# Swapped PSUM tags in one FFN, mixer norms by columns, operand sums inside the first group, a warm-up at the start, plain gates scaled a tile earlier, and the last but one root half a tile later

## The chip, the cores and the metric

The kernel runs on one core of a Trainium2 chip. The metric is the time of one execution on the device, in microseconds (us), less being better. A core has engines that run side by side, each with a queue of its own that it works through in order: TensorE (PE, matrix products out of SBUF into the PSUM banks; its weight loads are PEld), VectorE (DVE), ScalarE (ACT), GpSimd (POOL) and SyncE (SP, which here only issues loads and stores). They wait for each other through semaphores.

## The reference

Two blocks, each a half-weighted SwiGLU, a mixer and another half-weighted SwiGLU, all behind an RMSNorm; block 0 has mixer A (indexed sparse attention), block 1 mixer B (chunked gMLP). The sequence has 512 tokens of width 1024, the hidden width is 2816, all float32:

```
for i in range(2):
    h = h + 0.5 * swiglu(rmsnorm(h, norm_g[i, 0]), ffn_w_in[i, 0], ffn_w_out[i, 0])
    hn = rmsnorm(h, norm_g[i, 1])
    y = mixer_a(hn, ...) if i == 0 else mixer_b(hn, ...)
    h = h + y
    h = h + 0.5 * swiglu(rmsnorm(h, norm_g[i, 2]), ffn_w_in[i, 1], ffn_w_out[i, 1])
return rmsnorm(h, final_g)

def rmsnorm(x, g):  return x * rsqrt(mean(x * x) + EPS) * g
def swiglu(x, w_in, w_out):
    gate, up = split(x @ w_in)
    return (silu(gate) * up) @ w_out
```

## The kernel before

**Layout.** The activations stand transposed: `H[0..7]`, eight tiles of 128 features x 512 tokens. Every product is made of three matmuls on split operands: `xh`/`whi` hold the upper part of a number, `xl`/`wlo` the rest, and `mul3` (lines 366 to 368) issues hi x hi, lo x hi, hi x lo. Weights come in on SP's queue as `raw` (512 KB a load); ACT writes `whi` (line 183), DVE then `wlo` (line 186). The converted weights stand in a ring of three units of eight 128x128 pieces, so a unit's conversion waits until PE has left the unit three back.

**One FFN.** The first `group` makes four output tiles at once (gate and up of hidden tiles 0 and 1) in four banks, over eight slices k of the input: twelve matmuls a slice. Four `single`s make the gates and ups of hidden tiles 2 and 3 (banks `rest`). These two pairs of tiles are the "plain" ones: `plain_pairs` multiplies the gates by the norm's factor (DVE), applies Silu (ACT), and leaves the multiplication with the up tile and the split into `yh`, `yl` in a list `later`, of which `step` takes one. All other hidden tiles come from `two_pairs`, which forms a 2x2 block product from seven products instead of eight; its right-hand operands are sums of quarters of x that `sums(kp)` makes for kp = 0..3: two scalings into `m` (ACT, line 446), four subtractions into `u` (DVE, lines 448 to 451), a split into `th` (ACT, line 388) and `tl` (DVE, line 389). The products' banks are copied out at line 519 (ACT, into `u` and `m`). Then the output products follow, in groups and singles; `add` multiplies a finished bank by half the norm's factor (DVE line 642, `gate`), adds it to `h` (643), and the next stage's `xh`, `xl` and the sum of squares `sqacc` are made from it.

**PSUM.** Two tags, `acc` and `aux`, of four banks each. A new bank of a tag takes over the bank of that tag used longest ago and waits for its readers. The first FFN of block 1 ends on `acc` banks and the stage behind it begins on `acc` banks, as does the first FFN of block 1 behind the second of block 0.

**Norms.** The four FFNs use `scale_columns` (line 394: `sqacc` as the weights against one column of ones, so that token sums stand as four columns; a root of twelve small DVE operations) and `scale_rows` (line 402: back to a row per token, copied to `b` and to half of it, `rh`). The mixers use `token_scale` (lines 345 to 351: split `sqacc` into `ah` and `al`, two 512-column products, and a root on 128x512 tiles) and `as_columns`.

**Where x is built.** In FFN (0,0) `H` is still loading during the first group, and `behind` (lines 305 to 317) makes each slice's `xh`, `xl` and squares between the matmuls. There the sums follow one by one behind the singles; in the other three FFNs they stand in the first group at k = 5, 6, 7 and behind the first single.

**Order.** Nothing reorders: each engine works in the order in which the code issues its instructions. The last stage stores a 128-token tile at a time: `rest` (lines 1146 to 1151, two halves) and `store` (its root and its scaling, line 1161).

Of the kernel before, what the change touches and what calls it, by code (L numbers as in the profile page):

```python
# [19 lines left out]
P = 128  # L20
# [220 lines left out]
def tile_trunk(ctx: ExitStack, tc, specs_out, xT, wst, gT, gl, rel, onehot, bu, bv, lng, lnb, wspT, bsp, out):  # L241
# [21 lines left out]
    def bank(tag="acc"):  # L263
        return psum.tile([P, 512], F32, tag=tag, bufs=4, name=uname(tag))
# [5 lines left out]
    pad(const, 32)  # L270
    pad(small, 32)
# [68 lines left out]

    def token_scale(tag="aux"):

        ah = small.tile([P, S], F32R, tag="s0_512", bufs=1, name=uname("ah"))
        al = small.tile([P, S], F32R, tag="s1_512", bufs=1, name=uname("al"))
        nc.scalar.activation(ah, acc[0], AF.Copy)
        nc.vector.tensor_tensor(al, acc[0], ah.bitcast(F32), op=ALU.subtract)
        ps = bank(tag)
        mm(ps, ones_r, ah, start=True, stop=False)
        mm(ps, ones_r, al, start=False, stop=True)
        v = small.tile([P, S], F32, tag="ms", bufs=1, name=uname("ms"))  # L350
        nc.vector.tensor_scalar(v, ps, 1.0 / D, EPS, op0=ALU.mult, op1=ALU.add)
        return rsqrt(v, [P, S])

    def as_columns(rb):

        ps = bank("aux")
        for t in range(NT):
            nc.tensor.transpose(ps[:, t * P:(t + 1) * P], rb[:, t * P:(t + 1) * P], ident)
        c = small.tile([P, NT], F32, tag="rcol", bufs=1, name=uname("rcol"))
        nc.vector.tensor_copy(c, ps.rearrange("p (t q) -> p t q", q=P)[:, :, 0])  # L360
        return c

    def mul3(ps, w, x, first, last, **kw):
# [26 lines left out]

    def scale_columns(ps):

        for t in range(NT):
            mm(ps[:, t:t + 1], acc[0][:, t * P:(t + 1) * P], ones[:, :1], start=True, stop=True)
        v = small.tile([P, NT], F32, tag="vcol", bufs=1, name=uname("vcol"))
        nc.vector.tensor_scalar(v, ps[:, :NT], 1.0 / D, EPS, op0=ALU.mult, op1=ALU.add)
        return rsqrt(v, [P, NT])

    def scale_rows(rc, ps):
# [4 lines left out]
        rh = small.tile([P, S], F32, tag="ms", bufs=1, name=uname("rh"))  # L404
        nc.scalar.activation(rb, ps, AF.Copy)
        nc.scalar.activation(rh, ps, AF.Copy, scale=0.5)  # L406
        return rb, rh

    def ffn(layer, which, norm, finish, begin=None, hooks=None, aside=None, last=None):

# [6 lines left out]
        NJ = DFF // P  # L417
        KP = KD // 2
        n1, n2 = slice(0, HALF), slice(HALF, S)
        with tc.tile_pool(name=uname("ffn"), bufs=1) as fp:  # L420
# [59 lines left out]
            def step():  # L480
                for _ in range(min(1, len(later))):
                    later.pop(0)()
# [74 lines left out]
            def scale():  # L557
                R["ps"] = R.get("ps") or bank("aux")
                R["c"] = scale_columns(R["ps"])

# [4 lines left out]
            def hook(k):  # L565
                if hooks:
                    hooks[k]()
                elif k in (5, 7):
                    (scale if k == 5 else spread)()
                if k > 4 and not hooks:  # L570
                    sums(k - 5)
# [4 lines left out]
            rest = [bank("aux") for _ in range(2)]  # L576
            if not hooks:
                plain_pairs(banks, g[0])
            else:
                R["ps"] = bank("aux")  # L580
            single(rest[0], 2, KD, spec_in)
            sums(0) if hooks else sums(3)
            step()
# [5 lines left out]
            rest.append(bank("aux"))  # L589
            single(rest[2], 3, KD, spec_in)  # L590
            if hooks:
                spread()
                nc.vector.tensor_tensor(g[1][:, 0], rest[0], R["b"], op=ALU.mult)
                plain_pairs(banks, g[0])
                sums(2)
            step()
            rest.append(bank("aux"))
            single(rest[3], NJ + 3, KD, spec_in)
            if hooks:
                sums(3)  # L600
            flush()
            done, n_dp = 0, 0
            for ci, dps in enumerate(CHUNKS):
# [6 lines left out]
                for i in range(dps):  # L610
                    pair = PLAIN + 2 * n_dp
                    between = ()
                    if n_dp == 0:
                        between = [lambda: plain_pairs(rest, g[1], 1 if hooks else 0)]
                    if aside:
                        aside(n_dp)
                    if last and n_dp == sum(CHUNKS) - 1:
                        between = last[0](bank("acc"), gate_tile)
                    two_pairs(pair, "aux" if n_dp % 2 else "acc", between)
                    n_dp += 1  # L620
                flush()
                n_k = done - p0
                tag0 = "aux" if n_dp % 2 else "acc"
                tag1 = "acc" if n_dp % 2 else "aux"

# [55 lines left out]
    def mixer_a(dist, next_norm):  # L681
# [9 lines left out]
        with ExitStack() as stack:  # L691
# [11 lines left out]

            def scale():
                R["b"] = token_scale("acc")

            kw = bank()
            pq = [bank("aux") for _ in range(4)]
            group([kw] + pq, ["kw"] + [QI0 + P * i for i in range(4)], KD, spec_a, hooks={4: scale})
            rb = R["b"]  # L710
# [38 lines left out]
            with tc.tile_pool(name="mixai", bufs=1) as ip:  # L749
# [21 lines left out]
                for i, _ in enumerate(projections(range(1), "acc")):  # L771
                    if i != KD:
                        continue
                    rc = R["c"] = as_columns(rb)
                    nc.vector.tensor_scalar(rq, rc, P ** -0.5, None, op0=ALU.mult)
# [171 lines left out]
    def mixer_b(next_norm):  # L947
        with tc.tile_pool(name="mixb", bufs=1) as bp:
# [12 lines left out]
            with tc.tile_pool(name="mixbv", bufs=1) as vp:  # L961
# [8 lines left out]
                nc.gpsimd.affine_select(out=wT, in_=wT, compare_op=ALU.is_ge, fill=0.0, base=0,  # L970
                                        pattern=[[0, GROUPS], [1, P]], channel_multiplier=-1)
                for c in range(6):
                    tag = "aux" if c % 2 else "acc"
                    banks = [bank(tag) for _ in range(NT)]
                    for k in range(KD):
                        wh, wl = W.take(*[("b_w_in", (0,), k * P, [(0, BH + c * 512 + i * P, P)]) for i in range(4)])
                        for t in range(NT):
# [3 lines left out]
                            mm(banks[t], xh, wl, start=False, stop=k == KD - 1)  # L981
                        if c == 0 and k == 4:
                            R["b"] = token_scale()
                        if c == 0 and k == KD - 1:
                            R["c"] = as_columns(R["b"])
                        if c == 1 and k == 3:
# [110 lines left out]
    ffn(0, 1, 2, into(3))  # L1097
    ffn(1, 0, 3, into(4))
    mixer_b(5)


# [24 lines left out]
    def last_product(n_k, spec, y_parts, rc, temp):  # L1126
# [110 lines left out]
```

## Time and profile before

| | |
|---|---|
| median of 3 runs | 2111.97 us (2110.95 to 2118.17) |
| profiled execution, own time | 2112.86 us |
| its span (first to last instruction) | 2110.8 us |
| PE busy | 2076.8 us (98% of the span), 12208 matmuls |
| DVE busy | 1487.5 us (70%), 2044 instructions |
| ACT busy | 891.3 us (42%), 1151 instructions |
| POOL busy | 78.8 us (4%), 58 instructions |
| DMA | 209.7 MB, 99 GB/s on the mean |

The own time is 2.06 us more than the span; that part lies around the instructions. A matmul is counted busy from its start to the end of its drain, so that consecutive matmuls overlap; what one costs PE is the distance between starts.

### The profile page before, as it was taken

Reading aid. Unit: us, or ns where it says so; the run is one execution under the profiler, and the core shown is the slowest. Engines: PE = TensorE matmul, PEld = TensorE weight load, DVE = VectorE, ACT = ScalarE, POOL = GpSimd, SP = SyncE. Lnnn points to the kernel's source line nnn. Section 1 sums busy time; section 2 is a strip of 40 time slices with the busy share of each in tenths; the row PEclk is TensorE's granted clock in tenths of the full one; section 3 lists DMA queues with packets and bytes.
Section 4 is the critical chain, followed back from the end, with each engine's and each line's share of the span. In section 5 each row is a group of like instructions: output and inputs, shape, how many; then the busy total and the mean of one; then the engine's idle time right before and its main releaser. Section 6 shows DMA issues by size and latency. Waiting matters only on the chain.

```text
span 2110.8 us, 29664 instructions
## 1 busy us (share of the span) xinstructions
PE 2076.8 (98%) x12208; PEld 1839.1 (87%) x12208; DVE 1487.5 (70%) x2044; ACT 891.3 (42%) x1151; POOL 78.8 (4%) x58
## 2 busy tenths in 40 slices
PE   8999999999999999999999999999999999999998
PEld 6889898788888999897889999788888888989897
DVE  6868686697767677676868677645746466768686
ACT  5535344434445345344625344322323245435253
POOL 0000000143200000000000000000000000000000
PEclk9999999999999999999999999999999999999999
DMA  4233332222122222222323222422232222323221
GB/s 172 97 116 109 110 110 99 90 96 94 61 80 100 100 100 101 100 100 80 108 95 117 100 101 80 141 100 80 91 109 80 91 90 90 108 93 110 104 96 70
DMA packets 58887, 209.70 MB, mean 99 GB/s; under 512 B 6696, under 2 KB 6760, under 8 KB 58624
## 3 DMA queue, kind: packets, MB, share of 16 engines
q1 hardware_dynamic: 55584, 198.73, 26.9%
q0 software_dynamic: 1440, 5.41, 0.8%
q10 hardware_dynamic: 1728, 3.67, 0.5%
q8 instruction: 95, 1.56, 0.3%
q14 instruction: 40, 0.33, 0.1%
HBM read 205.67 MB, written 4.74 MB: 100 GB/s over the span
## 4 chain that ended last, share of the span: by engine, by line
PE 88%; DVE 7%; ACT 3%; issue 2%; DMA 0%; ACTq 0%; DVEq 0%; POOLq 0%
PE acc L366 15%; PE acc L367 15%; PE acc L368 15%; PE aux L366 10%; PE aux L367 10%; PE aux L368 10%; DVE wlo L186 1%; ACT whi L183 1%; PE aux L979 1%; PE aux L980 1%; PE aux L981 1%; PE aux L1031 1%; PE acc L979 1%; PE acc L980 1%; PE acc L981 1%
## 5 line engine op out<-in xcount | busy, mean ns | idle before, releaser
L186 DVE TENSOR_TENSOR wlo<-raw,whi 128x1024 fp32r<-128x1024 f32 (+1 forms) x382 | 464.2, 1219 | 309.7 <-ACT whi L183 308.2
L183 ACT ACTIVATE whi<-raw 128x1024 fp32r<-128x1024 f32 (+1 forms) x409 | 426.5, 1050 | 485.1 <-PE acc L367 203.7
L366 PE MATMUL acc<-xh,whi 128*128 128x256 f32 (+1 forms) x888 | 305.7, 344 | 8.9 <-ACT xh L305 5.9
L367 PE MATMUL acc<-xl,whi 128*128 128x256 f32 (+1 forms) x888 | 296.4, 334 | 0.1
L368 PE MATMUL acc<-xh,wlo 128*128 128x256 f32 (+1 forms) x888 | 296.3, 334 | 0.0
L366 PEld LDWEIGHTS acc<-xh,whi 128*128 128x128 f32 x888 | 169.5, 191 | 27.5 <-ACT xh L305 5.9
L366 PE MATMUL aux<-xh,whi 128*128 128x256 f32 (+1 forms) x592 | 190.7, 322 | 1.2 <-ACT rh L406 1.2
L368 PE MATMUL aux<-xh,wlo 128*128 128x256 f32 (+1 forms) x592 | 190.5, 322 | 1.3 <-DVE wlo L186 1.3
L367 PE MATMUL aux<-xl,whi 128*128 128x256 f32 (+1 forms) x592 | 190.2, 321 | 0.0
L366 PE MATMUL acc<-th,whi 128*128 128x256 f32 x640 | 181.8, 284 | 7.5 <-ACT u L519 6.0
L367 PEld LDWEIGHTS acc<-xl,whi 128*128 128x128 f32 x888 | 169.5, 191 | 18.2 <-issue 1.4
L368 PEld LDWEIGHTS acc<-xh,wlo 128*128 128x128 f32 x888 | 169.3, 191 | 16.7
L367 PE MATMUL acc<-tl,whi 128*128 128x256 f32 x640 | 181.2, 283 | 0.4 <-DVE tl L389 0.4
L368 PE MATMUL acc<-th,wlo 128*128 128x256 f32 x640 | 181.1, 283 | 0.0
L366 PE MATMUL aux<-th,whi 128*128 128x256 f32 x512 | 144.9, 283 | 0.0
L367 PE MATMUL aux<-tl,whi 128*128 128x256 f32 x512 | 144.9, 283 | 0.0
L368 PE MATMUL aux<-th,wlo 128*128 128x256 f32 x512 | 144.9, 283 | 0.0
L366 PEld LDWEIGHTS acc<-th,whi 128*128 128x128 f32 x640 | 122.8, 192 | 8.5 <-ACT u L519 6.8
L366 PE MATMUL acc<-yh,whi 128*128 128x512 f32 x328 | 127.7, 389 | 0.0
L367 PE MATMUL acc<-yl,whi 128*128 128x512 f32 x328 | 127.7, 389 | 0.0
L366 PE MATMUL aux<-yh,whi 128*128 128x512 f32 x328 | 127.6, 389 | 0.0
L367 PE MATMUL aux<-yl,whi 128*128 128x512 f32 x328 | 127.6, 389 | 0.0
(296 smaller groups left out, 4383.1 us busy)
## 6 DMA issues: line engine op xcount, KB each, us to landing
raw<-in_wst SPq DMA_DIRECT2D x372, 512.0 KB, 3.3
dist<-dist_rows ACTq DMA_DIRECT2D x8, 320.0 KB, 4.3
h<-in_xT SPq DMA_DIRECT2D x8, 256.0 KB, 6.8
tb<-dist POOLq DMA_DIRECT2D x8, 256.0 KB, 3.8
bias<-in_bv POOLq DMA_DIRECT2D x1, 1536.0 KB, 7.5
raw<-in_wst SPq DMA_DIRECT2D x2, 256.0 KB, 3.3
wT<-in_wspT POOLq DMA_DIRECT2D x1, 512.0 KB, 9.3
bs<-in_bsp POOLq DMA_DIRECT2D x1, 512.0 KB, 11.3
```

The lines of the kernel that those rows point to most:

```text
L183: self.nc.scalar.activation(hi[:, s], src[:, s], AF.Copy)
L186: self.lo_engine.tensor_tensor(lo[:, s], src[:, s], hi[:, s].bitcast(F32), op=ALU.subtract)
L366: mm(ps, wh, xh, start=first, stop=False, **kw)
L367: mm(ps, wh, xl, start=False, stop=False, **kw)
L368: mm(ps, wl, xh, start=False, stop=last, **kw)
L979: mm(banks[t], xh, wh, start=k == 0, stop=False)
L980: mm(banks[t], xl, wh, start=False, stop=False)
L981: mm(banks[t], xh, wl, start=False, stop=k == KD - 1)
L1031: mm(ps[:, t * P:(t + 1) * P], V[t][:, d * P:(d + 1) * P], wT[:, g, :], start=True, stop=True)
```

## The change

Six edits. (1) `ffn` takes a pair of tags, and the first FFN of block 1 gets them swapped. (2) The mixers' norm is made by `norm_hooks`, with `scale_columns` and `scale_rows`, in the first group at k = 4, 5 and 6; `scale_columns` itself multiplies the split parts `ah` and `al` by two columns of ones, where it multiplied the unsplit `sqacc` by one. (3) In FFN (0,0) `sums(0..3)` is issued in the first group at k = 4..7. (4) 24 matmuls of 128 columns on a tile of ones stand ahead of everything on PE; the load of `g_sb` goes from POOL's queue to ACT's; a spare region grows. (5) `plain_pairs` is cut in two: `plain_gates` (DVE) runs as soon as its banks are there, the Silu one tile later; those of the second pair come before the first `two_pairs` instead of in its middle. (6) In the last stage `store(2)` comes behind the first half of tile 3.

```diff
+WARM = 24
-    nc.gpsimd.dma_start(g_sb, gT)
+    nc.scalar.dma_start(g_sb, gT)
+    warm = bank("aux")
+    for _ in range(WARM):
+        mm(warm[:, :P], ones_r, ones_r, start=True, stop=True)
-    def token_scale(tag="aux"):
...
-    def as_columns(rb):
...
+    def parts_of_squares():
+        ah = small.tile([P, S], F32R, tag="s0_512", bufs=1, name=uname("ah"))
+        al = small.tile([P, S], F32R, tag="s1_512", bufs=1, name=uname("al"))
+        split(acc[0], ah, al)
+        return ah, al
-    def scale_columns(ps):
+    def scale_columns(ps, parts):
         for t in range(NT):
-            mm(ps[:, t:t + 1], acc[0][:, t * P:(t + 1) * P], ones[:, :1], start=True, stop=True)
+            for part in parts:
+                mm(ps[:, 2 * t:2 * t + 2], part[:, t * P:(t + 1) * P], ones_r[:, :2], start=part is parts[0],
+                   stop=part is parts[1])
+    def norm_hooks(R, ps, k):
...
+        return {k: parts, k + 1: columns, k + 2: rows}
-            def plain_pairs(banks, g, begun=0):
-                for i in range(begun, 2):
+            def plain_gates(banks, g):
+                for i in range(2):
                     nc.vector.tensor_tensor(g[:, i], banks[2 * i], R["b"], op=ALU.mult)
+            def plain_pairs(banks, g):
                 nc.scalar.activation(g, g, AF.Silu)
-            banks = [bank() for _ in range(4)]
+            banks = [bank(tags[0]) for _ in range(4)]
             if not hooks:
+                plain_gates(banks, g[0])
+            single(rest[0], 2, KD, spec_in)
...
+            else:
                 plain_pairs(banks, g[0])
+                sums(3)
             single(rest[1], NJ + 2, KD, spec_in)
             if hooks:
-                scale()
-                sums(1)
+                spread()
+                plain_gates(banks, g[0])
...
+            plain_gates(rest, g[1])
+            rest.append(bank(tags[1]))
+            single(rest[3], NJ + 3, KD, spec_in)
             step()
-            flush()
+            plain_pairs(rest, g[1])
-                    if n_dp == 0:
-                        between = [lambda: plain_pairs(rest, g[1], 1 if hooks else 0)]
-    ffn(1, 0, 3, into(4))
+    ffn(1, 0, 3, into(4), tags=("aux", "acc"))
-            store(t)
+                if (t, half) == (NT - 1, 0):
+                    store(t - 1)
+        store(NT - 1)
```

The order of DVE's instructions in the first group of FFN (0,0), from the slice of `h_76` on, before (`xl_94` and `xl_95` are the operands of slices k = 6 and 7, `wlo_308` the weights of a later unit):

```order
L306 SCALAR_TENSOR_TENSOR xl_93<-h_76,g_sb,xh_85 128x512
L317 TENSOR_TENSOR sqacc_171<-sqacc_171,sq_287 128x512
L306 SCALAR_TENSOR_TENSOR xl_94<-h_77,g_sb,xh_86 128x512
L317 TENSOR_TENSOR sqacc_171<-sqacc_171,sq_304 128x512
L186 TENSOR_TENSOR wlo_308<-raw_183,whi_307 128x1024
L306 SCALAR_TENSOR_TENSOR xl_95<-h_78,g_sb,xh_87 128x512
```

and of the change, where the sums' subtractions and splits stand between:

```order
L310 SCALAR_TENSOR_TENSOR xl_94<-h_77,g_sb,xh_86 128x512
L321 TENSOR_TENSOR sqacc_196<-sqacc_196,sq_343 128x512
L455 TENSOR_TENSOR u_36_348<-m_34_346 128x256
L456 TENSOR_TENSOR u_36_348<-m_35_347,m_34_346 128x256
L457 TENSOR_TENSOR u_37_349<-m_35_347,u_36_348 128x256
L458 TENSOR_TENSOR u_37_349<-m_35_347,u_37_349 128x256
L371 TENSOR_TENSOR tl_169<-u_36_348,th_165 128x512
L371 TENSOR_TENSOR tl_169<-u_37_349,th_165 128x512
L187 TENSOR_TENSOR wlo_361<-raw_208,whi_360 128x1024
L310 SCALAR_TENSOR_TENSOR xl_95<-h_78,g_sb,xh_87 128x512
```

Before, `xl_95` has one conversion of weights ahead of it behind `sqacc`; now it has a whole `sums` and that conversion, and `xl_94` likewise has `sums(0)` ahead of it.

The order of ACT's instructions in FFN (0,1), in the first `two_pairs` (`gate_5989` is the second plain pair, whose line 491 is the Silu), before:

```order
L519 ACTIVATE m_639_6174<-acc_6146 128x512
L183 ACTIVATE whi_6176<-raw_5924 128x1024
L183 ACTIVATE whi_6187<-raw_5999 128x1024
L491 ACTIVATE gate_5989<-gate_5989 128x1024
L519 ACTIVATE m_640_6222<-acc_6148 128x512
L183 ACTIVATE whi_6224<-raw_5926 128x1024
L475 ACTIVATE yh_6228<-gate_5989 128x1024
L519 ACTIVATE u_643_6255<-acc_6146 128x512
```

and of the change:

```order
L500 ACTIVATE gate_6035<-gate_6035 128x1024
L528 ACTIVATE m_643_6223<-acc_6195 128x512
L184 ACTIVATE whi_6225<-raw_5970 128x1024
L184 ACTIVATE whi_6236<-raw_6044 128x1024
L528 ACTIVATE m_644_6268<-acc_6197 128x512
L184 ACTIVATE whi_6270<-raw_5972 128x1024
L482 ACTIVATE yh_6274<-gate_6035 128x1024
L528 ACTIVATE u_647_6301<-acc_6195 128x512
```

The Silu of the second pair has gone from between the first two copies out of banks to ahead of both; `yh`, and the copy `u` behind it, stand where they stood.

The order of PE's matmuls where FFN (0,1) ends and FFN (1,0) begins, before (`acc_9052` is the first bank of the new FFN):

```order
L367 MATMUL acc_9007<-yl_8788,whi_8909 128x512
L368 MATMUL acc_9007<-yh_8787,wlo_8910 128x512
L366 MATMUL acc_9052<-xh_80,whi_8948 128x512
L367 MATMUL acc_9052<-xl_88,whi_8948 128x512
L368 MATMUL acc_9052<-xh_80,wlo_8949 128x512
```

and of the change:

```order
L349 MATMUL acc_9053<-yl_8834,whi_8955 128x512
L350 MATMUL acc_9053<-yh_8833,wlo_8956 128x512
L348 MATMUL aux_9098<-xh_80,whi_8994 128x512
L349 MATMUL aux_9098<-xl_88,whi_8994 128x512
L350 MATMUL aux_9098<-xh_80,wlo_8995 128x512
```

The matmuls are the same; the new FFN's first four banks are of the other tag.

## Rows read from the trace of the kernel before

**Rows 1.** Page, busy us of each engine, share of the span, instructions.
```profile
PE 2076.8 (98%) x12208; PEld 1839.1 (87%) x12208; DVE 1487.5 (70%) x2044; ACT 891.3 (42%) x1151; POOL 78.8 (4%) x58
```
**Rows 2.** Waits of PE: us in total, times, longest us.
```profile
PE acc L366 <- ACT u L519: 6.0, 4, 2.7
PE acc L366 <- ACT xh L305: 5.9, 1, 5.9
PE acc L366 <- DVE gate L642: 3.0, 2, 1.6
PE acc L979 <- DVE gate L642: 3.0, 2, 1.6
PE acc L366 <- ACT th L388: 1.5, 1, 1.5
PE aux L368 <- DVE wlo L186: 1.3, 3, 0.4
PE aux L366 <- ACT rh L406: 1.2, 1, 1.2
PE acc L349 <- DVE al L346: 0.8, 1, 0.8
PE acc L348 <- ACT ah L345: 0.8, 1, 0.8
```
**Rows 3.** PE's timeline at a boundary: start us, us, instruction, idle before and releaser.
```profile
975.39 0.39 PE L368 MATMUL acc<-xh,wlo 128*128 128x512 f32 x1
977.19 0.50 PE L366 MATMUL acc<-xh,whi 128*128 128x512 f32 x1 [1.42 <-DVE gate L642]
```
**Rows 4.** Windows: us; PE, PEld, DVE, ACT, POOL busy (x); clock; DMA share; GB/s.
```profile
3.00:18.50 15.50, 12.48 (x41) 9.45 (x42) 9.63 (x14) 9.72 (x16) 0.59 (x2) 1.00 1.00 365
20.20:32.20 12.00, 12.00 (x54) 9.31 (x54) 7.81 (x11) 6.27 (x10) 0.52 (x1) 1.00 0.35 119
383.70:387.10 3.40, 3.40 (x10) 2.63 (x9) 3.23 (x6) 0.00 (x0) 0.00 (x0) 0.50 0.35 134
1332.60:1336.00 3.40, 3.40 (x9) 2.63 (x8) 3.40 (x6) 2.19 (x3) 2.65 (x5) 0.50 0.45 112
```
**Rows 5.** Timeline of the start: PE's slices k = 0 and 3, and DVE.
```profile
10.69 0.63 PE L367 MATMUL acc<-xl,whi 128*128 128x512 f32 x1
11.11 0.63 PE L368 MATMUL acc<-xh,wlo 128*128 128x512 f32 x1
...
17.55 0.50 PE L367 MATMUL acc<-xl,whi 128*128 128x512 f32 x1
...
16.75 0.75 DVE L306 SCALAR_TENSOR_TENSOR xl<-h,g_sb,xh 128x512 fp32r<-128x512 f32 x1
```
**Rows 6.** Groups of `sums`: busy us, mean ns of one, idle before.
```profile
L389 DVE TENSOR_TENSOR tl<-u,th 128x512 fp32r<-128x512 f32 x32 | 22.0, 689 | 1.6
L446 ACT ACTIVATE m<-h,g_sb 128x512 f32<-128x512 f32 x32 | 21.2, 710 | 0.0
L448 DVE TENSOR_TENSOR u<-m 128x256 f32<-128x256 f32 x16 | 6.7, 421 | 4.4 <-ACT m L446 4.4
```
**Rows 7.** ACT's timeline in FFN (0,1), first `two_pairs`.
```profile
680.42 1.06 ACT L491 ACTIVATE gate<-gate 128x1024 f32<-128x1024 f32 x1 [2.49 <-DVE gate L490]
683.86 0.58 ACT L519 ACTIVATE u<-acc 128x512 f32<-128x512 f32 x1
```
**Rows 8.** PE's timeline in FFN (0,1): columns and rows of the norm.
```profile
641.95 0.95 PE L394 MATMUL aux<-ones,sqacc 128*128 128x1 f32 x8
648.31 1.05 PE L402 MATMUL aux<-ident,nwy 128*128 128x128 f32 x8
```
**Rows 9.** Line 394: ns of one (least, median, most), first and last start.
```profile
L394 PEld LDWEIGHTS aux<-ones,sqacc x32: 188/192/193, 42.8 to 1766.3; 128*128 128x128 f32 x32
L394 PE MATMUL aux<-ones,sqacc x32: 169/250/250, 43.1 to 1766.3; 128*128 128x1 f32 x32
```
**Rows 10.** DVE's timeline near the end.
```profile
2102.49 0.74 DVE L1146 SCALAR_TENSOR_TENSOR turned<-acc,last_rh,turned 128x512 f32<-128x512 f32 x1
```

More of the change, by code (lines that the diff above doesn't have):

```diff
@@ L339, in prepare @@
             behind_it.pop(0)()
-    def token_scale(tag="aux"):
[L343 to L352, printed above, removed]
-    def as_columns(rb):
[L356 to L361, printed above, removed]
     def mul3(ps, w, x, first, last, **kw):
@@ L403, in scale_rows, with parts, columns, rows @@
         rb = small.tile([P, S], F32, tag="nwy512", bufs=1, name=uname("rb"))
-        rh = small.tile([P, S], F32, tag="ms", bufs=1, name=uname("rh"))
+        rh = small.tile([P, S], F32, tag="ms", bufs=1, name=uname("rh")) if halves else None
         nc.scalar.activation(rb, ps, AF.Copy)
-        nc.scalar.activation(rh, ps, AF.Copy, scale=0.5)
+        if halves:
+            nc.scalar.activation(rh, ps, AF.Copy, scale=0.5)
         return rb, rh
-    def ffn(layer, which, norm, finish, begin=None, hooks=None, aside=None, last=None):
+    def norm_hooks(R, ps, k):
+        def parts():
+            R["sq"] = parts_of_squares()
+        def columns():
+            R["c"] = scale_columns(ps, R["sq"])
+        def rows():
+            R["b"], _ = scale_rows(R["c"], ps, False)
+        return {k: parts, k + 1: columns, k + 2: rows}
+    def ffn(layer, which, norm, finish, begin=None, hooks=None, aside=None, last=None, tags=("acc", "aux")):
         NJ = DFF // P
         KP = KD // 2
+        tag_of = lambda i: tags[i % 2]
         n1, n2 = slice(0, HALF), slice(HALF, S)
@@ L567, in hook @@
                     hooks[k]()
[L568 to L571, printed above, removed]
-            banks = [bank() for _ in range(4)]
+                elif k == 5:
+                    scale()
+                elif k == 7:
+                    spread()
+                elif k == 3:
+                    R["sq"] = parts_of_squares()
+                if k > 3 + (not hooks):
+                    sums(k - 4 - (not hooks))
+            banks = [bank(tags[0]) for _ in range(4)]
             group(banks, [0, NJ, 1, NJ + 1], KD, spec_in, hooks={k: lambda k=k: hook(k) for k in range(KD)})
             g = [gate_tile() for _ in range(2)]
-            rest = [bank("aux") for _ in range(2)]
+            R["ps"] = R.get("ps") or bank(tags[1])
+            rest = [bank(tags[1]) for _ in range(2)]
             if not hooks:
-                plain_pairs(banks, g[0])
[L579 to L583, printed above, removed]
+                plain_gates(banks, g[0])
+            single(rest[0], 2, KD, spec_in)
+            if hooks:
+                R["sq"] = parts_of_squares()
+                scale()
+            else:
+                plain_pairs(banks, g[0])
+                sums(3)
             single(rest[1], NJ + 2, KD, spec_in)
             if hooks:
-                scale()
-                sums(1)
+                spread()
+                plain_gates(banks, g[0])
             step()
-            rest.append(bank("aux"))
+            rest.append(bank(tags[1]))
             single(rest[2], 3, KD, spec_in)
+            step()
             if hooks:
-                spread()
-                nc.vector.tensor_tensor(g[1][:, 0], rest[0], R["b"], op=ALU.mult)
                 plain_pairs(banks, g[0])
-                sums(2)
+            plain_gates(rest, g[1])
+            rest.append(bank(tags[1]))
+            single(rest[3], NJ + 3, KD, spec_in)
             step()
-            rest.append(bank("aux"))
-            single(rest[3], NJ + 3, KD, spec_in)
             if hooks:
-                sums(3)
-            flush()
+                step()
+            plain_pairs(rest, g[1])
             done, n_dp = 0, 0
@@ L618, in ffn @@
                         between = last[0](bank("acc"), gate_tile)
-                    two_pairs(pair, "aux" if n_dp % 2 else "acc", between)
+                    two_pairs(pair, tag_of(n_dp), between)
                     n_dp += 1
@@ L622, in ffn @@
                 n_k = done - p0
-                tag0 = "aux" if n_dp % 2 else "acc"
-                tag1 = "acc" if n_dp % 2 else "aux"
+                tag0 = tag_of(n_dp)
+                tag1 = tag_of(n_dp + 1)
                 def spec_out(k, c, p0=p0):
@@ L702, in mixer_a @@
             R = {}
-            def scale():
-                R["b"] = token_scale("acc")
-            kw = bank()
+            kw, ps = bank(), bank()
             pq = [bank("aux") for _ in range(4)]
-            group([kw] + pq, ["kw"] + [QI0 + P * i for i in range(4)], KD, spec_a, hooks={4: scale})
+            group([kw] + pq, ["kw"] + [QI0 + P * i for i in range(4)], KD, spec_a, hooks=norm_hooks(R, ps, 4))
             rb = R["b"]
@@ L971, in mixer_b @@
                                         pattern=[[0, GROUPS], [1, P]], channel_multiplier=-1)
+                hooks = norm_hooks(R, bank("aux"), 4)
                 for c in range(6):
@@ L981, in mixer_b @@
                             mm(banks[t], xh, wl, start=False, stop=k == KD - 1)
[L982 to L985, printed above, removed]
+                        if c == 0 and k in hooks:
+                            hooks[k]()
                         if c == 1 and k == 3:
```

13 lines of the change are left out of this document (7 added, 6 removed).

## The prediction

> **What bounds the kernel now.** I read the page first: PE is busy for 98% of the span and no other engine for more than 70% [rows 1], so the time is PE's own work plus the places where PE stands or runs slowly. The second view is the list of PE's waits [rows 2]. Nearly all of it names places that the change touches: copies of the operand sums and products (`u`, `th`), the norm (`rh`, `al`, `ah`), a bank that is still being read (`gate`, line 642). The third view, the timeline, shows what a wait costs in full: between the last matmul before a boundary and the first behind it lie 977.19 − 975.39 = 1.80 us [rows 3], where a step of 512 columns takes 12.00 / 54 = 0.22 us [rows 4]. That is 1.58 us lost for a wait of 1.42, so each wait costs about 0.15 us of refilling beyond its length. The fourth view, the windows, has the clock: two stretches of 3.4 us run at 0.50, the lower of the two levels (1.2 instead of 2.4 GHz), one right behind the norm of mixer A (383.7), one behind the second boundary (1332.6) [rows 4]. A stretch of 3.4 us at half clock does 1.7 us of work, so it loses 1.7. In both, PE had stood for most of 2 us in short succession just before. By the same row of a full-clock step, the start runs at half clock too: steps of 0.42 us [rows 5].
>
> **The change part by part.** All sums are made against the profiled execution, 2112.86 us (2110.8 of span and 2.06 around it); the median of the runs shown is 0.9 lower.
>
> *First FFN, sums inside the first group.* Removed are the waits for `th` (1.5), for `rh` (1.2) and for the late `u` (2.7, the longest of the four of line 519) [rows 2]: 5.4 us, with three refills 5.9. Added is work for DVE and ACT in the group. One `sums` is four subtractions and two splits on DVE, 4 × 0.42 + 2 × 0.69 = 3.1 us (2.85 where they overlap at their ends, estimated), and on ACT two scalings (1.42) and two splits [rows 6]. PE's slice is twelve steps, 2.7 us. In 20.2 to 32.2 DVE has 12.00 − 7.81 = 4.2 us free and ACT 5.7 [rows 4], and three sums want 8.6 of DVE: this does not fit. Following both queues in their new order from slice 4 on: `xl` of slice 6 now stands behind `sums(0)`, which I make ready 0.9 us late; `xl` of slice 7 stands behind `sums(1)` and the conversion of a unit, 2.9 late in all; the columns need `al`, which stands behind the last two sums, 1.4 late. That is 5.2 lost in place of 5.9: **−0.7**. Bounds: all of it hidden, −5.9; nothing of 4 × 2.85 = 11.4 hidden, +5.5.
>
> *Other three FFNs, plain gates earlier.* The other three waits for `u` (6.0 − 2.7 = 3.3) and three for `wlo` (1.3) [rows 2] are 4.6, with six refills 5.5. ACT stood for 2.49 us at 680.42 because the Silu waited for its gate, with a copy and a conversion behind it, so that the copy `u`, for which PE waits, came at 683.86 [rows 7]. In the new order this Silu stands ahead of the first copies and its gate is computed during the single before; the copy moves up by the Silu's place, 1.06 us and what it waited. I reckon `u` about 0.3 us ahead of its use. The `wlo` waits come from a Silu and its table ahead of a conversion; that conversion now stands ahead of both. I leave 0.2 us: **−5.3**. Bounds 0 and −5.5.
>
> *Swapped banks.* The two boundaries cost 3.0 + 3.0 with four refills: 6.6 us [rows 2, 3]. With the other tag the first two banks are long free, so PE goes on, if weights and `xh` are there. What is late next is the conversion of the next unit on DVE, behind the same `gate` and `h` operations; stepping that queue on from the freed bank I estimate its slack at 0.9 us at the first boundary and 0.5 at the second. **−6.6**, bounds 0 and −6.6. Without the pause the stretch of half clock at 1332.6 has no cause left: **−1.7** (bounds 0 and −1.7).
>
> *Mixers' norm.* In mixer A `ah` and `al` cost 0.8 + 0.8 and two refills [rows 2], 1.9 us; now they are made at k = 4 and used a slice (five banks, 3.4 us) later. The half clock behind them goes too, 1.7. PE's work: out go two steps of 512 columns (0.45) and four transposes (about half of the eight passes of line 402, 0.45); in come eight narrow matmuls and the rows: the same things take 0.95 and 1.05 us in FFN (0,1), about 0.15 less without their drain [rows 8], so 0.8 + 0.9. Sum −1.9 − 1.7 − 0.9 + 1.7 = **−2.8**. In mixer B the work is likewise +0.8, and its waits are none of the nine largest, so at most 0.8: **+0.3**. Bounds for both: −3.6 and +1.6. The long root on 128x512 tiles that DVE loses costs nothing now, since no wait of rows 2 names it.
>
> *Warm-up.* It lets the first three slices run at full clock instead of half, thirteen steps worth 0.20 us each, 2.6 us. But the fourth slice needs its `xl`, made by DVE from 16.75 to 17.50, and PE starts on it at 17.55 [rows 5]. That `xl` stands behind the fourth unit's conversion, and in 3.0 to 18.5 the DMA engines are busy for a share of 1.00 with 365 GB/s [rows 4]: data set that time, not PE. So **0**; bounds −2.6 (nothing else binds) and +1.7 (PE, done early, waits for slice 3 and falls to half clock once more). The 24 warm-up matmuls lie in the 5.9 us that PE waits at the start anyway [rows 2]. The Trainium skill ("TensorE: Matmul & The Clock Gate", What's actually happening) says that the clock is throttled by default and activity releases it, so by it the warm-up would bring those 2.6 us; rows 5 say that the slice behind would wait them away.
>
> *Tail.* DVE works off its backlog to the end, of which the last of the four halves' first operation starts at 2102.49 [rows 10]. Moving a root among them leaves DVE's work as it is and changes the end by the small wait ahead of that root, an estimate: **−0.1**, bounds ±0.5.
>
> Sum: −0.7 − 5.3 − 6.6 − 1.7 − 2.8 + 0.3 + 0 − 0.1 = −16.9. That gives 2096.0 for the profiled execution and **2095 us** on the scale of the median.
>
> **The rivals.** (R1) A new wait in place of the old one: the copy `u` is still late, since `yh` (1.06 us) and a conversion stand ahead of it as before [rows 7]. The three waits then stay, 3.3 + 0.45: 2099. For it: my slack is only 0.3 us. (R2) The clock: standing about 3 us for slice 7 in the first FFN, and for slice 3 behind the warm-up, brings PE to half clock twice, 2 × 1.7: 2098. For it: both stretches of rows 4; against it, the 2.7 us wait for `u` [rows 2] had no such stretch behind it. The skill's same page (Why this matters for your kernels) warns that idle gaps between bursts of matmuls cost throughput; the trace agrees at 383.7, where the clock is 0.50. (R3) The change doesn't do what it says at the boundaries: DVE's conversions or `xl` are as late as its `gate` was, and the wait is only renamed; +8.3 with the clock: 2103. (R4) The sums of the first FFN are hidden after all: 2090. (R5) The start is not held by slice 3 and the warm-up brings 2.6: 2092. (R6) The other side: narrow matmuls on split parts cannot overlap with their own weight loads. There are now 48 of them (six norms of eight); load and product of line 394 are 0.19 and 0.25 us [rows 9]; one behind the other, 0.44 instead of the 0.10 of rows 8 (0.8 / 8), they cost 48 × 0.34 = 16 us, 2111; at half clock, where 0.88 stand in place of 0.10, 37 us, 2132. It decides from about 0.45 us each. Against it: the eight of rows 8 take 0.95 us together.
>
> **How the numbers follow.** Forecast 0.47; R1 0.12; R2 0.15; R3 0.08; R4 0.10; R5 0.05; R6 0.03. R4 and R5 together end at 2087, R1 and R2 together with a part of R3 at 2105: the range is **2087 to 2105**, leaving out R6 and pile-ups of the rest. A measurement of this kernel can tell about 0.5%, here 10.6 us: faster means below 2101.4, slower above 2122.5. Faster hold the forecast, R1, R2, R4 and R5 where they come alone, less the mixtures of R1 to R3: 0.78. Same: R3, such mixtures and half of R6: 0.19. Slower: 0.03.
>
> **What would show each step right or wrong.** In the changed kernel's list of waits, the rows for `gate` at line 642 are gone and none for `wlo` or `xl` at the two boundaries stands in their place; `u` (the copy out of banks) has no more than a few tenths; `ah` and `al` are gone in the mixers; a wait for `xl` or `xh` of 2 to 3 us and one for `al` stand in the first group of the first FFN. The windows behind the norm of mixer A and behind the second boundary are at 1.00. The fourth slice of the start still begins its second product at about 17.5. Eight narrow matmuls take 0.8 to 1 us. The prediction is wrong above all if the first group's lateness is far from 5.2 us, its least certain term, or if the clock falls at a place where I have it full.

## The result, and the profile after

| | before | changed |
|---|---|---|
| median | 2111.77 us (4 runs) | 2093.89 us (4 runs, 2093.53 to 2094.24) |
| profiled execution, own time | 2112.86 | 2093.53 |
| its span | 2110.8 | 2091.7 |

The ratio is 0.9909, with a 95% interval of 0.9893 to 0.9926: about 0.9% faster, 18 us. The forecast was 2095, with 2087 to 2105.

The first view is the page's line of busy times, which answers to [rows 1]:

```profile
PE 2076.6 (99%) x12252; PEld 1844.4 (88%) x12252; DVE 1476.7 (71%) x2046; ACT 894.3 (43%) x1157; POOL 78.1 (4%) x57
```

PE has as much to do as before; the span shrank around it by 19.1 us. What went shows in the list of PE's waits (us in total, times, longest), which answers to [rows 2] and is complete down to 0.3 us:

```profile
PE aux L289 <- ACT ones_r L286: 2.9, 1, 2.9
PE acc L348 <- ACT xh L309: 1.6, 1, 1.6
PE acc L349 <- DVE xl L310: 1.1, 2, 0.8
PE acc L908 <- ACT pT L898: 0.3, 1, 0.3
```

Of [rows 2] the first wait for `xh` has become one for the warm-up's operand; every other one is gone: those for `gate`, for `u`, for `th`, `rh` and `wlo`, and the mixer's for `ah` and `al`. Three new ones stand in the first group of the first FFN. In PE's timeline:

```profile
2.91 3.68 PE L289 MATMUL aux<-ones_r 128*128 128x128 f32 x16 [2.91 <-ACT ones_r L286]
...
17.59 0.50 PE L349 MATMUL acc<-xl,whi 128*128 128x512 f32 x1
...
27.66 0.50 PE L349 MATMUL acc<-xl,whi 128*128 128x512 f32 x1 [0.28 <-DVE xl L310]
32.10 0.50 PE L348 MATMUL acc<-xh,whi 128*128 128x512 f32 x1 [1.60 <-ACT xh L309]
33.41 0.50 PE L349 MATMUL acc<-xl,whi 128*128 128x512 f32 x1 [0.81 <-DVE xl L310]
```

(The first row ends where the asked window did; all 24 warm-up matmuls are done when slice 0 begins, at 8.09.) The second row is the one that [rows 5] have at 17.55: in this execution the fourth slice starts as it did. The last three are slices k = 6 and 7, waiting for operands that stand behind the sums. And the windows (us; PE, PEld, DVE, ACT, POOL busy; clock; DMA share; GB/s) of the places that [rows 4] had at half clock, with a new one ahead:

```profile
34.00:37.40 3.40, 3.40 (x10) 2.62 (x9) 3.27 (x8) 2.58 (x5) 0.00 (x0) 0.50 0.73 289
380.00:383.40 3.40, 3.40 (x20) 2.90 (x18) 1.67 (x2) 0.33 (x1) 0.00 (x0) 1.00 0.36 124
1315.00:1319.00 4.00, 4.00 (x20) 3.30 (x19) 3.01 (x4) 1.38 (x2) 0.00 (x0) 1.00 0.18 63
```

Mixer A's norm (380) and the second boundary (1315) run at 1.00; the stretch behind the three waits (34.0) runs at 0.50.

**Where the 19.1 us came from.** Apart from the norms' and the warm-up's, PE's products are the same in both programs and in the same order, so each can be looked up in both timelines; the difference of its two starts is what has been gained by then.

| up to | start before | start after | gained here | forecast |
|---|---|---|---|---|
| fourth product of the first FFN's first `two_pairs` | 73.99 | 72.79 | 1.2 | 0.7 |
| mixer A, behind its norm | 402.19 | 398.06 | 2.9 | 2.8 |
| same product of FFN (0,1) | 684.49 | 678.64 | 1.7 | 1.8 |
| third bank of FFN (1,0) (boundary) | 979.79 | 970.38 | 3.6 | 3.3 |
| same product of FFN (1,0) | 1036.74 | 1025.22 | 2.1 | 1.8 |
| mixer B, fourth bank (boundary) | 1332.04 | 1316.93 | 3.6 | 3.3 |
| mixer B, 10 matmuls on (the clock) | 1336.01 | 1319.20 | 1.7 | 1.7 |
| FFN (1,1), first single | 1784.84 | 1767.40 | 0.6 | 0.3 (wlo) − 0.3 (mixer B) |
| same product of FFN (1,1) | 1808.19 | 1789.34 | 1.4 | 1.5 |
| end of the span | 2110.83 | 2091.68 | 0.3 | 0.1 |

### The profile page after: what moved, and what is told of

The parts are those of the page before. It is cut to its first block, busy times and chain, and to the rows that moved or that the text cites. A ratio compares the mean times of both kernels' runs of the same rounds, so it can differ in the third digit from the quotient of the medians.

```text
span 2091.7 us, 29771 instructions
## 1 busy us (share of the span) xinstructions
PE 2076.6 (99%) x12252; PEld 1844.4 (88%) x12252; DVE 1476.7 (71%) x2046; ACT 894.3 (43%) x1157; POOL 78.1 (4%) x57
## 4 chain that ended last, share of the span: by engine, by line
PE 97%; DVE 2%; ACT 1%; issue 0%; ACTq 0%; DVEq 0%
PE acc L348 16%; PE acc L349 16%; PE acc L350 16%; PE aux L348 12%; PE aux L350 12%; PE aux L349 12%; PE acc L990 1%; PE aux L992 1%; PE aux L990 1%; PE acc L992 1%; PE acc L991 1%; PE aux L991 1%; PE aux L1040 1%; PE acc L908 1%; PE aux L872 1%; PE aux L896 0%
## 5 line engine op out<-in xcount | busy, mean ns | idle before, releaser
L348 PE MATMUL acc<-xh,whi 128*128 128x512 f32 (+1 forms) x864 | 299.2, 346 | 1.7 <-ACT xh L309 1.6
L349 PE MATMUL acc<-xl,whi 128*128 128x512 f32 (+1 forms) x864 | 289.5, 335 | 1.1 <-DVE xl L310 1.1
L350 PE MATMUL acc<-xh,wlo 128*128 128x512 f32 (+1 forms) x864 | 289.1, 335 | 0.0
L350 PEld LDWEIGHTS acc<-xh,wlo 128*128 128x128 f32 x864 | 164.8, 191 | 16.9
L348 PE MATMUL acc<-th,whi 128*128 128x256 f32 x608 | 172.4, 284 | 0.0
L350 PE MATMUL acc<-th,wlo 128*128 128x256 f32 x608 | 172.1, 283 | 0.0
L349 PE MATMUL acc<-tl,whi 128*128 128x256 f32 x608 | 172.0, 283 | 0.0
L348 PE MATMUL aux<-th,whi 128*128 128x256 f32 x544 | 154.0, 283 | 0.0
L349 PE MATMUL aux<-tl,whi 128*128 128x256 f32 x544 | 154.0, 283 | 0.0
L350 PE MATMUL aux<-th,wlo 128*128 128x256 f32 x544 | 154.0, 283 | 0.0
L350 PE MATMUL acc<-yh,wlo 128*128 128x512 f32 x328 | 127.6, 389 | 0.0
```

Source lines behind the costliest of these rows:

```text
L348: mm(ps, wh, xh, start=first, stop=False, **kw)
L349: mm(ps, wh, xl, start=False, stop=False, **kw)
L350: mm(ps, wl, xh, start=False, stop=last, **kw)
```

## Experiments

Each was made from the changed kernel unless it says otherwise. Where a median is of one run, its profile carries the reading. Runs of the kernel before beside them gave medians of 2112.7 to 2113.8, up to 2 us above the 2111.77 of the result. The intervals of e1, e2, e3, e5 and e7 overlap the change's own (0.9893 to 0.9926), so their differences of 1 to 5 us are read from the traces, place by place.

**The sums two slices later** (e1): where the first group's waits come from.

```diff
-                if k > 3 + (not hooks):
-                    sums(k - 4 - (not hooks))
+                if k > 5 - (not hooks):
+                    sums(k - 6 + (not hooks))
...
                 scale()
+                sums(2)
...
                 plain_gates(banks, g[0])
+                sums(3)
```

> The changed kernel with the operand sums of the first FFN two slices later: two in the first group at k = 6 and 7, behind the operands of slices 6 and 7, one behind each of the first two singles. Theory A (the queue order alone makes those operands late, and the wait then lowers the clock): the three waits of the first group (0.28, 1.60 and 0.81 us) and the half clock from 34.0 to 37.4 (1.7) go, with refills about 5.3 us, and nothing comes in their place: about 2088.6 us. Rival B (DVE's and ACT's work does not fit, wherever it stands): the loss moves to th, tl or rh behind the singles, and the time stays within 1.5 us of 2093.9.

Measured: 2091.38 us, ratio to the kernel before 0.9886 (0.9870 to 0.9902), 2.5 us better than the change. No stretch behind the first group is at half clock, and PE's timeline shows none of the three waits. Two others are there:

```profile
39.80 0.27 PE L384 MATMUL aux<-ones_r,al 128*128 128x2 f32 x1 [0.97 <-DVE al L371]
...
64.83 0.39 PE L348 MATMUL acc<-th,whi 128*128 128x256 f32 x1 [0.96 <-ACT m L528]
```

So A is right on the cause of the three waits, and B on part of the rest: 2.2 us of it, with refills, moved on to `al`, which stands behind the second sums on DVE, and to the copy `m`, which stands behind a `yh` and a Silu on ACT. By the end of the first group the change is 5.4 us behind the kernel before (its last product there starts at 37.35 instead of 31.95). This run has that back but for 1.0 us, lost at the start, where slice 3 begins its second product at 18.59 instead of 17.59 (see e2); 5.4 − 1.0 − 2.2 is the 2.2 us between the spans, 2091.7 and 2089.5.

**Without the warm-up, and with 10 matmuls of it** (e2, e3).

```diff
-WARM = 24
+WARM = 0        (e2)    WARM = 10        (e3)
```

> The changed kernel without the warm-up matmuls. Theory A (prediction: data set the start of slice 3, so the warm-up changes nothing): slice 3 begins its second product at 17.5 to 17.6 as before, 2093.9 within 0.5. Rival B (the warm-up holds slice 0 back to 8.09 and the conversion for slice 3 waits for PE to leave a unit): PE begins at about 5.3, at half clock to about 11, slice 1 begins at about 11.0 instead of 11.85, and the conversion starts with its load's landing, 13.7, or soon behind it, so 0.3 to 0.8 us faster.

> The changed kernel with 10 warm-up matmuls instead of 24. They take 10 x 0.213 us from 2.91, so they end at about 5.05, before the first operand is ready at 5.34. Theory A (data set slice 3): no change, 2093.9 within 0.5. Rival B (the warm-up's length holds slice 0 and with it the unit that slice 3's conversion needs): slice 1 begins at about 10.3, the conversion starts with the landing at 13.7 instead of 14.55, slice 3 is 0.8 us earlier, and the time 0.8 us less, 2093.1; if the clock rises as late as without a warm-up, half of that.

Measured: 2092.73 us without (0.9893, 0.9877 to 0.9909), 2092.67 with ten (0.9895, 0.9879 to 0.9912): both medians 1.2 us below that with 24. The timelines of ACT and PE in the run without:

```profile
13.98 1.06 ACT L184 ACTIVATE whi<-raw 128x1024 fp32r<-128x1024 f32 x1 [1.73 <-PE acc L349]
...
17.01 0.50 PE L349 MATMUL acc<-xl,whi 128*128 128x512 f32 x1
```

The change has the second at 17.59 and the first as

```profile
14.55 1.06 ACT L184 ACTIVATE whi<-raw 128x1024 fp32r<-128x1024 f32 x1 [2.33 <-PE acc L349]
```

In both the conversion waits for PE to leave a unit, not for its load: B. The warm-up took 8.09 − 2.91 = 5.2 us, 24 steps of 0.22, and slice 0, which starts at 5.48 without it, could not start before. Of the 1.2 us between the two profiled executions this start is 0.6. The rest arose in the first group, where the clock stayed up without the warm-up (1.6 us) and PE then waited for `al` (1.0 and a refill). With ten, slice 3 gained 0.2 instead of 0.8 us; the full clock came at about 12.0 there, at 11.5 in the run without. That execution is the slowest of its four (2094.49), with 6.8 us at half clock in the first group.

Nor is 17.59 what the warm-up always gives. In the nine traces with 24 warm-up matmuls (the change's, e1, e4, e5, e8 to e12) slice 0 starts at 8.1, PE's steps fall from 0.43 to 0.23 us somewhere between 9.9 and 12.5, and slice 3's second product follows at 17.53 to 18.73. The earliest (e5) and the latest (e12):

```profile
17.53 0.50 PE L349 MATMUL acc<-xl,whi 128*128 128x512 f32 x1
```
```profile
18.73 0.50 PE L349 MATMUL acc<-xl,whi 128*128 128x512 f32 x1
```

In the three without any (e2, e7, e13) the steps fall between 9.9 and 11.5, and that product starts at 16.90 to 17.02. So no run shows that the warm-up brings the full clock forward; it shows that slice 0 is held back, and the change's own execution is one of the two luckiest of the nine.

**The sums back behind the singles** (e5): is the change's place for them better than the old one, now that the gates are moved?

```diff
-                if k > 3 + (not hooks):
-                    sums(k - 4 - (not hooks))
+                if k > 4 and not hooks:
+                    sums(k - 5)
...   (sums(0) to sums(3) behind singles 0 to 3, as in the kernel before)
```

> The changed kernel with the first FFN's operand sums back behind the four singles, as in the kernel before. Theory A (the prediction's account: waits of 5.4 for rh, th and u return, the first group's 5.5 go): about 0.7 to 1.2 us slower, 2094.6 to 2095.1. Rival B (the 2.7 us wait for u came from the Silu's place, which stays as in the change, not from the sums): only rh and th return, about 3.2 with refills, and the time is about 2 us less than 2093.9, near 2091.7.

Measured: 2096.93 us (0.9913, 0.9894 to 0.9933), 3.0 slower than the change. PE's timeline where the sums are first used:

```profile
64.99 0.58 PE L348 MATMUL acc<-th,whi 128*128 128x256 f32 x1 [5.12 <-ACT th L370]
```

Neither theory had this. The wait for `u` is indeed gone, as B says, but the one for `th` is not the old 1.5 us: it is 5.1, and 6.6 us at a clock of 0.51 follow it. The last sums now stand in ACT's queue behind the first pair's `yh`, which itself waits for DVE's multiplication of its gate; in the kernel before they stood ahead of both.

```profile
61.54 1.06 ACT L482 ACTIVATE yh<-gate 128x1024 fp32r<-128x1024 f32 x1 [4.85 <-DVE gate L504]
```

So this run is not quite the old order, and it leaves open what the old place would give with these sums ahead of `yh`.

**One part of the change undone at a time** (e4, e8): the swapped tags, and the plain gates' order in the other three FFNs.

```diff
-    ffn(1, 0, 3, into(4), tags=("aux", "acc"))
+    ffn(1, 0, 3, into(4))                          (e4)
```

> The changed kernel with the tags of the first FFN of block 1 not swapped. Theory A (each boundary waits for a bank that DVE still reads, and the second wait lowers the clock): the four waits of 1.4 to 1.6 us come back, 6.6 to 6.8 us with refills, and with them about 1.7 us of half clock behind the second boundary: about 2102.3 us. Rival B (the swap only uncovers another lateness of DVE's, so that little of this was gained by it): less than 4 us slower, under 2098.

Measured: 2104.63 us, 10.7 slower. PE's waits again have

```profile
PE acc L348 <- DVE gate L655: 3.1, 2, 1.6
PE acc L990 <- DVE gate L655: 3.1, 2, 1.6
```

and the windows behind both boundaries are at half clock, where the kernel before had it behind the second only:

```profile
975.00:978.40 3.40, 3.40 (x9) 2.63 (x8) 3.40 (x6) 2.19 (x3) 0.00 (x0) 0.50 0.00 0
1326.60:1330.00 3.40, 3.40 (x10) 2.63 (x9) 3.40 (x6) 2.19 (x3) 2.43 (x5) 0.50 0.40 105
```

A, with one more stretch of clock. (0.6 us of the 10.7 arose ahead of both, at the start and in the first group.) For e8, the gates of each pair are multiplied right with the Silu and the second pair goes back into the first `two_pairs`:

```diff
             if not hooks:
                 plain_gates(banks, g[0])
+                plain_pairs(banks, g[0])
...
+                    if n_dp == 0 and not hooks:
+                        between = [lambda: (plain_gates(rest, g[1]), plain_pairs(rest, g[1]))]
```

> The changed kernel with the plain gates of the other three FFNs in the place and order of the kernel before (the first FFN as in the change). Theory A (the waits for u and for wlo came from this order): in each of the three, PE again loses about 0.58 for wlo and 1.24 for u, 5.5 to 6.2 in all: about 2099.7 us. Rival B (the swapped order of columns or the split parts of the norm freed them): under 2 us slower.

Measured: 2100.35 us, 6.5 slower, with these waits of PE beside the change's own:

```profile
PE acc L348 <- ACT u L528: 2.5, 2, 1.4
...
PE aux L348 <- ACT u L528: 1.1, 1, 1.1
...
PE aux L350 <- DVE wlo L187: 0.8, 2, 0.4
PE acc L350 <- DVE wlo L187: 0.4, 1, 0.4
```

Those are the waits of [rows 2]: A.

**The mixers' norm by rows again** (e9, e10).

```diff
-            group([kw] + pq, ..., hooks=norm_hooks(R, ps, 4))
+            group([kw] + pq, ..., hooks={4: scale})        (token_scale and as_columns back, in both mixers)
```

> The changed kernel with the norm of both mixers by rows, as in the kernel before. Theory A (mixer A's two waits of 0.8 us and the half clock behind them come back, 1.9 + 1.7, less 0.8 of PE's work; mixer B gains 0.2): about 2.5 us slower, 2096.4. Rival B (the half clock was chance and the waits alone count): about 0.9 us slower, 2094.8.

Measured: 2107.45 us, 13.6 slower, which is none of the theories. At mixer A PE waited for `ah` and `al` as before, and the products there start 1.6 us later; 1.1 more went in a wait for `wi` behind it. The other 11 us came in small pieces throughout the program: PE's 5535 steps of 512 columns took 230.3 ns on the mean instead of 226.9, and its 6080 of 256 columns 118.8 instead of 120.1 (distances between the starts of consecutive matmuls, gaps over 300 ns left out). The tile `rcol` that comes back with `as_columns` takes 16 bytes, and the spare region had been widened by 32 in the change; so the same again, with the old region:

```diff
-    pad(small, 64)
+    pad(small, 32)
```

> The run with the mixers' norm by rows again, but with the spare region of the small pool at 32 bytes as in the kernel before, instead of 64. That run was 13.7 us longer, of which only about 2 lie at mixer A's norm; through the whole program its steps of 512 columns are 3.4 ns longer and those of 256 columns 1.3 ns shorter. Theory A (the tile rcol that came back moved every later tile by 32 bytes, and the longer spare region makes up for it in the change): with 32 the steps are those of the change again (226.9 and 120.1 ns), and the time is 2 to 2.9 us over it, 2096 to 2097. Rival B (the steps changed for another reason, such as the added instructions): the time stays near 2107.

Measured: 2097.25 us, 3.4 slower than the change, with steps of 226.9 and 120.1 ns again: A. At mixer A the norm costs 3.0 us here (the other 0.4 arose at the start) and 1.6 in e9. Both runs have the same two waits of 0.8 us there, but not the same window behind them (e9 first, then e10):

```profile
381.00:384.40 3.40, 1.80 (x7) 1.09 (x7) 2.37 (x3) 0.92 (x2) 0.00 (x0) 1.00 0.20 65
```
```profile
383.40:386.80 3.40, 3.40 (x10) 2.66 (x9) 3.19 (x7) 0.00 (x0) 0.00 (x0) 0.50 0.25 100
```

**The spare region alone** (e11: 32 bytes, e12: 96, in the changed kernel).

> The changed kernel with the spare region of the small pool at 32 bytes, as in the kernel before; nothing else is altered. Theory A (the place in SBUF sets the length of a step): 5531 steps of 512 columns are 3.4 ns longer, 6080 of 256 columns 1.3 ns shorter, 18.8 - 7.9 = 10.9 us: about 2104.5. Rival B (the place doesn't matter): 2093.9.

> The changed kernel with the spare region at 96 bytes. Theory A (only the place within 64 bytes matters): as with 32 bytes, about 2104.5, with steps of 230.3 and 118.8 ns. Rival B (any other place is as good or as bad by its own measure): steps and time different from both 2093.9 and 2104.5 by over 2 us. Rival C (the place doesn't matter): 2093.9.

Measured: 2103.45 and 2104.33 us, with steps of 230.2 and 118.8 ns, and 230.3 and 118.8. Both A: 32 bytes either way cost 10 us, and the two places 64 bytes apart behave alike. Which steps grew shows in the groups of matmuls (busy us, mean ns of one; a matmul's own time moves with its step) of the change and, below, of the run with 32 bytes:

```profile
L348 PE MATMUL acc<-xh,whi 128*128 128x256 f32 x456 | 129.1, 283 | 0.0
L348 PE MATMUL acc<-yh,whi 128*128 128x512 f32 x328 | 127.7, 389 | 0.0
L348 PE MATMUL aux<-xh,whi 128*128 128x512 f32 x208 | 81.4, 392 | 0.0
```
```profile
L348 PE MATMUL acc<-yh,whi 128*128 128x512 f32 x328 | 129.7, 395 | 0.0
L348 PE MATMUL acc<-xh,whi 128*128 128x256 f32 x456 | 128.4, 281 | 0.0
L348 PE MATMUL aux<-xh,whi 128*128 128x512 f32 x208 | 81.4, 391 | 0.0
```

Products on `yh`, which lies behind the small pool, grew by 6 ns; those of 512 columns on `xh`, whose tiles lie ahead of it, did not.

**A better version** (e7): the sums later as in e1, no warm-up, the parts of the squares made ahead of the second sums, and the second Silu ahead of the first pair's `yh`.

```diff
                     hooks[k]()
+                    if k == KD - 1:
+                        R["sq"] = parts_of_squares()
...
             step()
+            plain_pairs(rest, g[1])
             if hooks:
                 step()
-            plain_pairs(rest, g[1])
```

> The changed kernel with no warm-up, the sums as in the run with the sums two slices later, the parts of the squares made ahead of the second sums (so that al is early), and the second Silu ahead of the first pair's yh on ACT. Theory A (the first FFN's losses are all lateness of one queue position each): against 2091.4 of the sums two slices later, the wait for al (0.97) and for m (0.96) go with two refills, 2.2 us, and the start gives 0.6: about 2088.6. Rival B (ACT and DVE are full there, and the waits only move on): no better than 2090.5.

Measured: 2089.06 us (0.9889, 0.9873 to 0.9906). The wait for `al` is gone and the start has its 0.6; the wait for `m` is still 0.9 us, so A failed there: moving the Silu ahead of `yh` did not free the copy. And last (e13), only the tiles behind `yh` in each FFN moved by 32 bytes, among them the second ring of converted weights:

```diff
-            pad(fp, 256)
+            pad(fp, 288)
```

> The best kernel so far (no warm-up, sums later, parts of the squares ahead, second Silu ahead of yh) with 32 bytes more of spare region inside each FFN, behind th, tl, yh and yl and ahead of the gates, the temporaries and the second ring of converted weights. In the runs with other spare regions, where all of these moved by 32 bytes, the steps of 512 columns on yh became 6 ns longer and those of 256 columns 1.3 ns shorter on the mean, with xh as well as with th. Theory A (the 256-column gain comes from the second ring of weights, the 512-column loss from yh): the 256-column steps are 118.8 ns, those of 512 columns stay at 226.9, 7.9 us less than 2089.1: about 2081. Rival B (the gain comes from th and tl, or from something else that stays put here): no change, 2089.

Measured: **2084.26 us** (0.9860, 0.9844 to 0.9877), the fastest here, 4.8 below e7 and 9.6 below the change. Steps: 227.0 ns for 512 columns, 119.3 for 256. Of the 1.3 ns that the 256-column steps gained with everything moved, 0.8 came with these tiles, 0.8 x 6080 = 4.9 us; the rest belongs to what stayed put, which speaks for both theories in part. (The conversion for slice 3 waits for its load in this run, at 13.87:

```profile
13.87 1.06 ACT L184 ACTIVATE whi<-raw 128x1024 fp32r<-128x1024 f32 x1 [1.55 <-DMA raw<-in_wst]
```

that is how early the data let it start.)

## Why the prediction was right

The forecast of −16.9 against the profiled execution met −19.3 (2112.86 to 2093.53), and the terms hold in the table above to 0.6 us each; what they have of the clock and of the warm-up came out so partly by chance.

- *First FFN*, −0.7: −1.2 together with the start. Slices 6 and 7 were late by 0.85 and 2.85 us from start to start, where I had followed the queues to 0.9 and 2.9. The 1.4 us for `al` didn't come; in their place PE ran 3.4 us at half clock, lost 1.6, and so came too late to wait. Where the clock stayed up (e2, e4, e11, e12), the wait for `al` was there, 1.0 (`PE aux L384 <- DVE al L371: 1.0, 1, 1.0` in each). R2 thus came true in this one place, and replaced a term instead of adding to it. R4, all hidden, was wrong, and e1 shows that the place of the sums made most of it so: two slices later 2.2 us of waiting were left.
- *Other FFNs*, −5.3: about −5.9, and e8 gives them back. The margin was thinner than forecast: ACT ends the copy `u` at 677.94 + 0.58 = 678.52 in FFN (0,1), and PE starts the product that needs it at 678.64, 0.1 us later instead of 0.3; R1 missed by that much:

```profile
677.94 0.58 ACT L528 ACTIVATE u<-acc 128x512 f32<-128x512 f32 x1
...
678.64 0.32 PE L348 MATMUL acc<-th,whi 128*128 128x256 f32 x1
```

- *Swapped banks*, −6.6 and −1.7: −7.2 and −1.7; e4 gives them back. R3 fell: neither `wlo` nor `xl` is waited for there. The 1.7 is what the one execution of [rows 4] had: the prediction has PE standing for most of 2 us ahead of both slow stretches, but ahead of this one it was 3.0, as it was at the first boundary, where the clock stayed up (last section).
- *Mixers' norm*, −2.8 and +0.3: −2.9 and about 0. Eight narrow matmuls take 382.85 to 383.66 in mixer A, 0.81 us, as the row of the old ones said; R6 fell. (By its own figures R6 would have decided from 0.23 us each, 0.10 + (2101.4 − 2095) / 48, not from 0.45.) The 1.7 of clock in this term, too, is that of one execution: e9 has the waits without it, e10 with it.
- *Warm-up*, 0: the number held by luck, and the reason failed. I had its 24 matmuls lie in the 5.9 us of waiting; they began at 2.91, once their operand was there, and ended 2.6 us after slice 0 could have begun. And the fourth slice isn't set by data: its conversion waits for PE to leave a unit, so whatever PE loses early is lost there too. The data would have let that conversion start at about 13.9 (13.87 in e13, which does wait for its load) instead of 14.52, so about 0.7 of the 2.6 us was to be had at best. Over the nine traces slice 3 came up to 1.2 us later than in the kernel before (17.53 to 18.73 against 17.55), and 0.5 to 0.7 earlier without the warm-up. The Trainium skill's statement ("TensorE: Matmul & The Clock Gate", What's actually happening) that activity releases the throttle agrees with these traces in so far as each begins with steps of 0.43 us and goes over to 0.23 once PE has worked; that these 24 matmuls bring it forward, this case doesn't bear out.
- *Tail*, −0.1: −0.3; no run isolates it.

One step was missing. I gave the wider spare region no term, as if a step's length were fixed. It is not (e11): without that line the change would have come out at 2103.5, a gain of half the size, and the forecast 8 us off. Its term came out as nothing because the wider region makes up for `rcol`, which the change took out: the steps are those of the kernel before (226.9 and 120.1 ns in both). The load of `g_sb` on ACT's queue had no term either, and no run isolates it: without a warm-up slice 0 starts at 5.48 to 5.83 us, in the kernel before at 5.89.

## What to carry to other kernels

When PE is the bound, list its waits, follow the two or three queues behind each in the new order, and price each wait from start to start; that was good to 0.6 us a term here. Ask of each wait at the start what releases it: here it was PE itself, and a warm-up ahead of the first product held up that product and whatever hangs on it. A block of work put into a queue ahead of the operands of the next slice makes those late, however idle the engine is on the average; two slices later it cost 2.2 us instead of 5.3. After any edit that adds or removes a tile, compare the length of the commonest step with the old one before reading anything else: 32 bytes moved 10 us.

## What the runs showed that I had not expected

- The place of tiles in SBUF sets the step of a matmul: 32 bytes more or less behind the small pool made 512-column steps 230.2 instead of 226.9 ns, and 256-column steps 118.8 instead of 120.1. Why was not found.
- The clock doesn't answer to the same waits in the same way. Behind waits of 1.6 and 0.8 us in the first group it was at half for 3.4 us in the change, not at all without the warm-up, and for about 6.8 us with ten matmuls of it. The windows from 32.6 to 39.4 of the last two, in that order:

```profile
32.60:39.40 6.80, 6.57 (x29) 5.47 (x30) 6.42 (x15) 5.12 (x10) 0.00 (x0) 1.00 0.44 155
```
```profile
32.60:39.40 6.80, 6.17 (x15) 4.83 (x16) 6.52 (x14) 5.12 (x9) 0.00 (x0) 0.51 0.43 155
```

The kernel before had it already: PE waited 1.4 and 1.6 us at each of its boundaries, and the stretch behind the first ran at full clock (next row), that behind the second at half [rows 4]; in e4 both ran at half.

```profile
977.20:980.60 3.40, 1.77 (x7) 1.16 (x8) 3.37 (x6) 1.35 (x3) 0.00 (x0) 1.00 0.47 154
```

So one such place can cost a single profile up to 3.4 us of work (6.8 us at half clock), and a difference of that size is to be read place by place. What decides it is open.
